# Gate/up weights from six raw tiles, three of them lent, and second attention's weights prepared one tile at a time by whole-tile operations

## The chip, the cores and the metric

The kernel runs on one core of a Trainium2 chip. The metric is the device time of one launch in microseconds, the median of several runs; lower is better.

## The reference, cut to what matters

A two-layer decoder over 1024 tokens of width 1024, float32. Layer A is differential attention, layer B stick-breaking attention with keys and values of its own from the residual stream. Behind each attention stand an output projection and a SwiGLU feed-forward block of inner width 2816, each with root-mean-square norms before and after and a residual sum.

```python
def swiglu(h, w_gate_up, w_down):
    gate, up = jnp.split(h @ w_gate_up, 2, axis=-1)
    return (jax.nn.silu(gate) * up) @ w_down

kv = rms_norm(x, kv_norm_g) @ kv_w            # layer B: keys and values
q  = rms_norm(x, mix_pre_g[1]) @ b_w_q        # layer B: queries
x  = x + rms_norm(m @ b_w_o, mix_post_g[1])   # layer B: output projection
```

## The kernel before, in words

**Products.** Each float32 operand is cut into a rounded high part and a remainder, and every product is three matmuls (high by high, low by high, high by low) into one PSUM bank.

**Order of the work.** The kernel is written as threads (Python generators). A planner, `Weaver`, runs them against a clock of its own and gives every instruction its place in the queue of its engine; each engine then works strictly in that order on the chip, SyncE's queue of DMA issues (SP) too. The planner's costs stand in the code: three matmuls of 512 columns take 1536/2372 us (`pe_time`), a DVE operation of n columns (1.04 n + 70) ns, an ACT one (0.833 n + 52) ns, plus 93 ns with a scale from a tile. A load is thought to be there 2.6 us behind its issue of 1.0 us, and a store's tile free 2.4 us behind its own. Tiles come from pools (`Slots`): `acq` waits in the planner until one is free, `put` gives it back, `lend` and `unlend` move tiles from one pool to another for a time.

**Gate/up.** `phase_ffn` runs twice ("A", "B"). Its loop `gate_up` goes over 22 column blocks f. For each, seven operand combinations (order `MORD`, a Strassen-like scheme over gate and up weights and the two halves of the tokens) give seven products of 12 matmuls, 84 matmuls for one f. `take` adds each product from its bank to half tiles `e` on DVE, `gated` makes silu(gate) times up, and `store` writes the result to DRAM (`act`).

**Gate/up's weights.** One `QuadJob` for each f. `loader` acquires three tiles of the pool `S_raw` (two are loaded with gate and up weights of 512 KB each, one is work space) and spawns `quad`. That makes seven split weight tiles `w` (pool `S_w`, nine tiles): DVE forms the combinations that need one (two as `raw<-raw`, three as `raw<-raw,raw`), ACT casts the high part, POOL subtracts to get the low part. Only when all seven are done do the three raw tiles go back. `S_raw` has three tiles, so the loads of the next f stand behind the last POOL subtraction of this f.

**Second attention's weights.** `pre_weights` prepares 32 weight tiles for layer B while feed-forward A runs: 24 with a gain for each 128-column block (queries, keys, values) and 8 without (`wo`). Each job takes two of the five tiles of pool `S_tr` (`tr`; the norms between stages use the same tiles), loads 512 KB, splits and stores both parts to DRAM (`prebq`, `prebk`, `prebv`, `prewo`). With a gain, the split is 8 ACT and 8 DVE operations of 128 columns. The next job is begun 1.0 + 2.6 + 13.5 us of the planner's time behind the last, so two jobs can be in work.

**Down.** `down` follows gate/up with 22 split rows of the down weight (`Job`, also through `S_raw`), its sums in tiles `acc` and `e`.

Of the kernel before, what the change touches and what calls it, by code (L numbers as in the profile page):

```python
# [13 lines left out]
AF = mybir.ActivationFunctionType  # L14
ALU = mybir.AluOpType
# [3 lines left out]
P = 128  # L19
# [3 lines left out]
NC = D // P  # L23
# [10 lines left out]
MORD = (3, 5, 4, 2, 6, 7, 1)  # L34
# [207 lines left out]
def acq(*homes):  # L242
    return ("acq", homes)


def delay(t):
    return ("delay", t)
# [10 lines left out]
def ACT(n, extra=0):  # L258
    return ("act", (0.833 * n + 52 + 93 * extra) / 1e3)


def DVE(n, rate=1.04):
    return ("dve", (rate * n + 70) / 1e3)
# [6 lines left out]
def SP(x=0.62):  # L270
    return ("sp", x)
# [17 lines left out]
def yoco_trunk(  # L289
# [7 lines left out]
    W = Weaver()  # L297
    pe, act, dve, pool, sp = [InOrder(tc, e) for e in (nc.tensor, nc.scalar, nc.vector, nc.gpsimd, nc.sync)]
# [8 lines left out]
    def tiles(pl, n, shape, dt, name):  # L307
        return [pl.tile(shape, dt, name=f"{name}{i}") for i in range(n)]
# [13 lines left out]
    S_raw = Slots(tiles(cpool, 3, [P, 1024], F32, "raw"))  # L322
    S_tr = Slots(tiles(cpool, 5, [P, 1024], F32, "tr"))
# [7 lines left out]
    oB = drp.tile([D, T], F32, name="oB")  # L331
    actd = [drp.tile([P, T], F32, name=f"act{f}") for f in range(NF)]

    S_half, S_trx = Slots(), Slots()

    def halves(t):
        return [t[:, :512], t[:, 512:]]
# [47 lines left out]
    pres = []  # L385

    def pre_weights(ready):
        yield ready
        yield delay(25.0)

        def work(job, raw, hi):
            if job.gain is not None:
                g_ev, g = job.gain()
                yield g_ev
            h = hi.t.bitcast(F32R)
            if job.gain is not None:
                for c in range(NC):
                    cs = slice(c * P, c * P + P)
                    yield ACT(P, 1)
                    act.activation(h[:, cs], raw.t[:, cs], AF.Copy, scale=g[:, c:c + 1])  # L400
                for c in range(NC):
                    cs = slice(c * P, c * P + P)
                    yield DVE(P + 58)
                    dve.scalar_tensor_tensor(raw.t[:, cs], raw.t[:, cs], g[:, c:c + 1], hi.t[:, cs],
                                             op0=ALU.mult, op1=ALU.subtract)
            else:
                yield ACT(1024)
                act.copy(h, raw.t)
                yield DVE(1024)
                dve.tensor_tensor(raw.t, raw.t, hi.t, op=ALU.subtract)  # L410

            def store(x, cs):
                yield SP(1.0)
                sp.dma_start(out=job.d[:, cs], in_=x.t)
                yield delay(2.4)
                W.put(x)
                W.set(job.ev)

            W.spawn(store(hi, slice(0, 1024)), 60, "prest")
            W.spawn(store(raw, slice(1024, 2048)), 60, "prest")  # L420

        for job in pres:
            raw = yield acq(S_tr)
            hi = yield acq(S_tr)
            yield SP(1.0)
            sp.dma_start(out=job.view(raw.t), in_=job.src)
            yield delay(2.6)
            W.spawn(work(job, raw, hi), 60, "pre" + job.name)
            yield delay(13.5)

    def loader():
        queue = []
# [86 lines left out]
        def load(k_, job):  # L519
            yield turn[k_]  # L520
            home = job.home if job.home is not None else S_w
            sh = yield acq(home)
            sl = yield acq(home)
            W.set(turn[k_ + 1])
            yield job.pre.ev
            for x, cs in ((sh, slice(0, 1024)), (sl, slice(1024, 2048))):
                yield SP(1.0)
                sp.dma_start(out=f32(x.t), in_=job.pre.d[:, cs])
            yield delay(2.6)
            job.h, job.l = sh, sl  # L530
            W.set(job.ev)

        for k, job in enumerate(jobs):
            W.cur.prio = -2 if k > 3 else 3
            if isinstance(job, LoadJob):
                if job.after is not None:
                    yield job.after
                W.spawn(load(k, job), -2, "load" + job.name)
                continue
            if isinstance(job, QuadJob):  # L540
                rr = []
                for src in job.srcs:
                    raw = yield acq(S_raw)
                    yield SP(1.0)
                    sp.dma_start(out=cview(raw.t)[0], in_=src.rearrange("(c p) n -> p c n", p=P))
                    rr.append(raw)
                rr.append((yield acq(S_raw)))
                yield delay(2.6)
                W.spawn(quad(k, job, *rr), plan("p.splitg", 20), "quad" + job.name)
                yield delay(-2.6)  # L550
                continue
            if job.after is not None:
                yield job.after
            raw = yield acq(S_raw)
            n = 0
            for src, view in job.srcs:
                yield SP(1.0 if len(job.srcs) == 1 else 0.5)
                dst, n = view(raw.t)
                sp.dma_start(out=dst, in_=src)
            yield delay(2.6)  # L560
            W.spawn(split(k, job, raw, n), plan("p.split" + job.name[0], 20) if k > 3 else -3, "split" + job.name)
            yield delay(-2.6)
# [266 lines left out]
    hA, hFA, hB, hFB = Hid(), QuadHid(), Hid(), QuadHid()  # L829
    phase_done = {k: Ev() for k in ("A", "woA", "ffnA", "B", "woB", "ffnB")}  # L830
# [746 lines left out]
    def phase_ffn(nm, st, before, hin, xsrc, xdst, g_post, hout):  # L1577
# [7 lines left out]
        def opener():  # L1585
            yield phase_done[before]
            gL, plL = phase_pool("ffl" + nm)
            W.give(S_act, tiles(plL, 4, [P, 1024], F32R, "fa"))
            gG, plG = phase_pool("gu" + nm, "right")
            own = tiles(plG, 6, [P, 4, 512], F32R, "hx")  # L1590
            W.spawn(hin.combine(own), -20, "combine")
            W.spawn(scratch(), -20, "scratch")
            W.set(opened)
            yield gu_done
            gG.__exit__(None, None, None)
            g, pl = phase_pool("dn" + nm, "right")
            acc.extend(tiles(pl, 2, [P, D], F32, "acc"))
            for x in hin.e:
                v = x.rearrange("p a b -> p (a b)")
                acc.extend([v[:, :1024], v[:, 1024:]])  # L1600
            stv["gpost"] = pl.tile([P, D], F32, name="gpostf")
            stv["junk"] = pl.tile([P, 1024], BF16, name="junkf")
            W.give(S_act, tiles(pl, 8, [P, 1024], F32R, "fb"))
            stv["gev"] = Ev()
            W.spawn(load_bcast(stv["gpost"], g_post, stv["gev"]), 6)
            W.set(dn_open)
            yield left
            g.__exit__(None, None, None)
            hin.gE.__exit__(None, None, None)
            gL.__exit__(None, None, None)  # L1610
            W.set(phase_done["ffn" + nm])

        W.spawn(opener(), -30, "open")
        W.spawn(hin.ready(), 0, "ready")

        def scratch():
            for i, x in ((6, hin.e[2]), (7, hin.e[1]), (1, hin.e[0])):
                yield hin.op_ev[i]
                v = x.rearrange("p a b -> p (a b)")
                W.give(S_sg, [v[:, k * 512:(k + 1) * 512] for k in range(4)])  # L1620
# [499 lines left out]
    def main():  # L2120
        W.spawn(warm_up(), 0, "warm")
        W.spawn(first_norm(), -37, "first")
        W.spawn(loader(), -2, "loader")
        W.spawn(load_gA(), -13, "gA")
        W.spawn(load_gB(), 35, "gB")
        W.spawn(phase_A(), -77, "A")
        W.spawn(phase_wo("A", sA, "A", oA, x_in, xd[0], mix_post_g[0], ffn_pre_g[0], hFA, eA), 49, "woA")
        W.spawn(load_early(eA, "A", oA, lambda m: [oA_ev[h][m // 4] for h in range(7)], sA), -47, "earlyA")
        W.spawn(wo_early("A", sA, eA), 75, "earlyMM")
        W.spawn(wo_early("B", sB, eB), 81, "earlyMM")  # L2130
        W.spawn(phase_ffn("A", fA, "woA", hFA, xd[0], xd[1], ffn_post_g[0], hB), 26, "ffnA")
        W.spawn(pre_weights(phase_done["woA"]), 60, "pre")
        W.spawn(phase_B(), 1, "B")
        W.spawn(phase_wo("B", sB, "B", oB, xd[1], xd[2], mix_post_g[1], ffn_pre_g[1], hFB, eB), -5, "woB")
        W.spawn(load_early(eB, "B", oB, lambda m: [oB_ev[p][m // 2] for p in range(7)], sB), -41, "earlyB")
        W.spawn(phase_ffn("B", fB, "woB", hFB, xd[2], out_f, ffn_post_g[1], None), -80, "ffnB")
        return
        yield
# [40 lines left out]
```

## Time and profile before

| | us |
|---|---|
| median of 3 runs | 2670.67 (2669.65 to 2674.35) |
| profiled execution, own time | 2676.72 |
| its span, first to last instruction | 2674.9 |

PE is the matmul engine, DVE the vector, ACT the scalar engine, POOL GpSimd, SPq the queue that issues the DMAs. All helpers record one source line, so groups are told apart by their tiles: `bank<-hT,w` and `bank<-hx,w` are gate/up's matmuls (48 and 36 for one f), `bank<-w,fa` and `bank<-w,fb` the down product's, `tr<-tr,gB` the preparation of second attention's weights. Behind a group stands the idle time of its engine just before it and, after `<-`, what ended that.

### The profile page before, as it was taken

What the parts mean: (1) busy time and instruction counts of PE and PEld (TensorE: products, weight loads), DVE (VectorE), ACT (ScalarE), POOL (GpSimd) and SP (SyncE); (2) the same over time, 40 slices, a digit from 0 to 9 for tenths busy, and PEclk for the clock granted to TensorE, in tenths of its full rate; (3) what the DMA queues carried; (4) which work ended last, traced back from release to release, by engine and by line L of the source; (5) the groups of instructions that cost most, each with busy time, mean ns of one, the idle gap of its engine ahead of it and who ended that gap; (6) DMA issues with size and microseconds to landing.
All of it is one profiled execution on the core that took longest, in us unless ns stands there. A gap on an engine that the chain in (4) does not pass through costs nothing. (4 is left out here: it accounts for less than half of the span.)

```text
span 2674.9 us, 36855 instructions
## 1 busy us (share of the span) xinstructions
PE 2549.2 (95%) x12771; PEld 2153.7 (81%) x12771; DVE 1857.0 (69%) x3351; ACT 1189.3 (44%) x2710; POOL 776.2 (29%) x713
## 2 busy tenths in 40 slices
PE   8999999897999999899999999999989999999998
PEld 8998999675887777688878888887767888888887
DVE  4767676866766666676768887888777655564667
ACT  4555555644444444331146655556454333332111
POOL 2111111334444444323210000000044545453331
PEclk9999999998999999999999999999999999999999
DMA  6333333441444444555454344444542232324233
GB/s 168 87 80 80 92 76 97 127 163 55 142 155 152 157 150 142 205 189 185 154 195 110 104 118 113 116 116 127 189 144 78 81 95 71 95 71 152 100 102 127
DMA packets 259258, 331.55 MB, mean 124 GB/s; under 512 B 20992, under 2 KB 179072, under 8 KB 259072
## 3 DMA queue, kind: packets, MB, share of 16 engines
q1 hardware_dynamic: 259072, 329.20, 40.1%
q8 instruction: 101, 1.65, 0.3%
q14 instruction: 85, 0.70, 0.1%
HBM read 197.67 MB, written 81.13 MB: 104 GB/s over the span
## 5 line engine op out<-in xcount | busy, mean ns | idle before, releaser
L283 PE MATMUL bank<-hT,w 128*128 128x512 f32 x3264 | 814.1, 399 | 26.0 <-ACT w L283 12.9
L283 PEld LDWEIGHTS bank<-hT,w 128*128 128x128 f32 x3264 | 607.7, 191 | 158.8 <-ACT w L283 18.3
L283 POOL TENSOR_TENSOR w<-raw,w 128x512 fp32r<-128x512 f32 (+1 forms) x343 | 522.1, 1539 | 514.8 <-ACT w L283 450.6
L283 PE MATMUL bank<-hx,w 128*128 128x512 f32 x1584 | 367.6, 389 | 4.7 <-DVE hx L283 4.7
L283 DVE TENSOR_TENSOR e<-e,bank 128x512 f32<-128x512 f32 x360 | 240.7, 680 | 187.1 <-ACT e L283 100.0
L283 PEld LDWEIGHTS bank<-hx,w 128*128 128x128 f32 x1584 | 296.9, 188 | 68.3 <-DVE hx L283 6.9
L283 PE MATMUL bank<-w,hT 128*128 128x384 f32 (+1 forms) x1728 | 344.6, 346 | 4.8 <-DMA w<-prewo 2.6
L283 ACT CAST w<-raw 128x512 fp32r<-128x512 f32 x308 | 188.1, 618 | 353.2 <-DVE raw L283 222.9
L283 PE MATMUL bank<-w,fb 128*128 128x512 f32 x1344 | 311.5, 389 | 1.2 <-POOL w L283 1.0
L283 PEld LDWEIGHTS bank<-w,hT 128*128 128x128 f32 x1728 | 299.7, 189 | 15.0 <-DMA w<-prewo 3.1
L283 PEld LDWEIGHTS bank<-w,fb 128*128 128x128 f32 x1344 | 252.0, 188 | 54.3 <-POOL w L283 1.5
L283 DVE TENSOR_TENSOR e<-bank,e 128x512 f32<-128x512 f32 x224 | 151.8, 687 | 90.5 <-PE bank L283 87.9
L283 PE MATMUL bank<-ident,tr 128*128 128x128 f32 x1059 | 163.6, 282 | 42.8 <-DVE tr L283 22.3
L283 PE MATMUL bank<-w,fa 128*128 128x512 f32 x768 | 186.0, 396 | 11.1 <-DVE e L283 5.9
L283 PEld LDWEIGHTS bank<-ident,tr 128*128 128x128 f32 x1059 | 129.8, 145 | 76.1 <-DVE tr L283 25.9
L283 PEld LDWEIGHTS bank<-w,fa 128*128 128x128 f32 x768 | 145.9, 191 | 43.7 <-ACT e L283 5.2
L283 POOL MEMSET atB<- 128x128 f32 x128 | 25.1, 205 | 504.3 <-PE bank L283 499.4
L283 POOL TENSOR_SCALAR w<-raw 128x1024 fp32r<-128x1024 f32 x48 | 68.9, 1435 | 300.3 <-PE bank L283 210.2
L283 DVE TENSOR_TENSOR raw<-raw 128x512 f32<-128x512 f32 x88 | 59.5, 713 | 120.7 <-DMA raw<-in_ffn_w_gate_up_dram 120.7
L283 POOL TENSOR_TENSOR sm<-sm,nhalf 128x1 f32<-128x1 f32 (+1 forms) x72 | 57.7, 802 | 291.0 <-DVE sm L283 291.0
L283 DVE TENSOR_TENSOR_SCAN rB<-rB,zeroB 128x512 f32<-128x512 f32 (+3 forms) x144 | 134.9, 951 | 7.8 <-ACT rB L283 6.9
L283 DVE TENSOR_TENSOR raw<-raw,raw 128x512 f32<-128x512 f32 x132 | 131.8, 998 | 0.0
(210 smaller groups left out, 3618.8 us busy)
## 6 DMA issues: line engine op xcount, KB each, us to landing
raw<-in_ffn_w_gate_up_dram SPq DMA_DIRECT2D x88, 512.0 KB, 5.1
xy<-st SPq DMA_DIRECT2D x192, 128.0 KB, 2.3
act<-e SPq DMA_DIRECT2D x88, 256.0 KB, 5.5
raw<-in_ffn_w_down_dram SPq DMA_DIRECT2D x44, 512.0 KB, 4.5
xyB<-stB SPq DMA_DIRECT2D x176, 128.0 KB, 4.2
fb<-act SPq DMA_DIRECT2D x28, 512.0 KB, 4.4
raw<-in_a_w_qkv_dram SPq DMA_DIRECT2D x96, 128.0 KB, 2.6
tr<-x SPq DMA_DIRECT2D x22, 512.0 KB, 4.1
```

What stands on the lines that cost most here:

```text
L283: return tc.keep_in_program_order(f(*a, **k))
```

## The change

The gate/up jobs may take their raw tiles from `S_raw` or from a new pool `S_rx`. In each feed-forward block, once all seven operands of the tokens are ready, three of the five `tr` tiles are lent to `S_rx`, and they go back when gate/up ends. `pre_weights` now starts at that same point rather than 25 us behind the end of the output projection. With two `tr` tiles left it has one job in work. A job with a gain is now one DVE multiplication of 1024 columns in place, then, as for one without, one ACT cast and one DVE subtraction of 1024 columns. Its pause falls from 13.5 to 11.0 us.

```diff
-    S_half, S_trx = Slots(), Slots()
+    S_half, S_trx, S_rx = Slots(), Slots(), Slots()
 ...
     def pre_weights(ready):
-        yield ready
-        yield delay(25.0)
+        for ev in ready:
+            yield ev
 ...
             if job.gain is not None:
-                for c in range(NC):
-                    cs = slice(c * P, c * P + P)
-                    yield ACT(P, 1)
-                    act.activation(h[:, cs], raw.t[:, cs], AF.Copy, scale=g[:, c:c + 1])
-                for c in range(NC):
-                    cs = slice(c * P, c * P + P)
-                    yield DVE(P + 58)
-                    dve.scalar_tensor_tensor(raw.t[:, cs], raw.t[:, cs], g[:, c:c + 1], hi.t[:, cs],
-                                             op0=ALU.mult, op1=ALU.subtract)
-            else:
-                yield ACT(1024)
-                act.copy(h, raw.t)
+                v3 = raw.t.rearrange("p (c n) -> p c n", c=NC)
                 yield DVE(1024)
-                dve.tensor_tensor(raw.t, raw.t, hi.t, op=ALU.subtract)
+                dve.tensor_tensor(v3, v3, g.unsqueeze(2).broadcast_to([P, NC, P]), op=ALU.mult)
+            yield ACT(1024)
+            act.copy(h, raw.t)
 ...
+            yield DVE(1024)
+            dve.tensor_tensor(raw.t, raw.t, hi.t, op=ALU.subtract)
 ...
-            yield delay(13.5)
+            yield delay(11.0)
 ...
-                    raw = yield acq(S_raw)
+                    raw = yield acq(S_raw, S_rx)
 ...
-                rr.append((yield acq(S_raw)))
+                rr.append((yield acq(S_raw, S_rx)))
 ...
+            bookR = []
+            W.spawn(lend_raw(bookR), -20, "lendraw")
             W.set(opened)
             yield gu_done
+            W.unlend(bookR)
 ...
+        def lend_raw(book):
+            for i in MORD:
+                yield hin.op_ev[i]
+            yield from W.lend(S_tr, S_rx, 3, whole, book)
 ...
-        W.spawn(pre_weights(phase_done["woA"]), 60, "pre")
+        W.spawn(pre_weights([hFA.op_ev[i] for i in MORD]), 60, "pre")
```

## Rows read from the trace of the kernel before

**Rows 1.** The page, busy time and share of the span.
```profile
PE 2549.2 (95%) x12771; PEld 2153.7 (81%) x12771; DVE 1857.0 (69%) x3351; ACT 1189.3 (44%) x2710; POOL 776.2 (29%) x713
```

**Rows 2.** Windows by stage: length, busy by engine, PEclk, DMA share, GB/s.
```profile
785.76:1109.17 323.41, 301.64 (x1261) 240.04 (x1260) 219.85 (x343) 141.01 (x314) 150.15 (x108) 0.97 0.45 148
1109.17:1146.94 37.77, 26.71 (x96) 20.30 (x97) 20.65 (x31) 18.57 (x39) 7.26 (x5) 0.86 0.65 236
1146.94:1321.02 174.08, 174.08 (x769) 144.15 (x768) 127.08 (x171) 30.80 (x41) 54.73 (x29) 1.00 0.53 186
2028.67:2428.51 399.84, 399.84 (x1765) 331.08 (x1764) 229.29 (x315) 152.24 (x269) 212.34 (x147) 1.00 0.30 92
```

**Rows 3.** Timeline of PE, gate/up A: start, length, group.
```profile
728.52 11.04 PE L283 MATMUL bank<-hT,w 128*128 128x512 f32 x48
...
747.56 11.04 PE L283 MATMUL bank<-hT,w 128*128 128x512 f32 x48
...
893.48 0.73 PE L283 MATMUL bank<-hT,w 128*128 128x512 f32 x2 [1.69 <-ACT w L283]
...
1100.85 8.32 PE L283 MATMUL bank<-hx,w 128*128 128x512 f32 x36
```

**Rows 4.** Timeline of the DMA queue SP in gate/up A.
```profile
668.93 0.99 SPq L283 DMA_DIRECT2D raw<-in_ffn_w_gate_up_dram  x2
...
798.23 1.01 SPq L283 DMA_DIRECT2D raw<-in_ffn_w_gate_up_dram  x2
...
905.95 1.01 SPq L283 DMA_DIRECT2D raw<-in_ffn_w_gate_up_dram  x2
907.01 1.07 SPq L283 DMA_DIRECT2D tr<-in_kv_w_dram  x1
...
927.17 1.01 SPq L283 DMA_DIRECT2D raw<-in_ffn_w_gate_up_dram  x2
```

**Rows 5.** Waits of SP, 785.76 to 1099: total us, times, longest.
```profile
SPq L283 <- POOL w L283: 204.8, 14, 15.6
```

**Rows 6.** Timeline of all engines within one period of gate/up A.
```profile
911.93 1.29 DVE L283 TENSOR_TENSOR raw<-raw 128x512 f32<-128x512 f32 x2 [3.27 <-DMA raw<-in_ffn_w_gate_up_dram]
...
922.17 1.70 DVE L283 SCALAR_TENSOR_TENSOR tr<-tr,gB,tr 128x128 f32<-128x128 f32 x2
...
925.86 1.29 POOL L283 TENSOR_TENSOR w<-raw,w 128x512 fp32r<-128x512 f32 x1 [2.13 <-ACT w L283]
```

**Rows 7.** Groups of 785.76 to 1109.17: busy, mean ns, idle before.
```profile
L283 DVE SCALAR_TENSOR_TENSOR tr<-tr,gB,tr 128x128 f32<-128x128 f32 x120 | 77.6, 685 | 0.0
...
L283 ACT ACTIVATE tr<-tr,gB 128x128 fp32r<-128x128 f32 x120 | 43.3, 397 | 15.4 <-DMA tr<-in_kv_w_dram 11.4 <-DMA tr<-in_b_w_q_dram 3.9
```

**Rows 8.** 1024-column operations: DVE and ACT on tr (min/median/max ns), DVE on w.
```profile
L283 DVE TENSOR_TENSOR tr<-tr,tr x8: 1214/1218/1466, 1189.9 to 1316.4; 128x1024 f32<-128x1024 f32 x8
...
L283 ACT CAST tr<-tr x8: 1047/1053/1057, 1181.5 to 1310.6; 128x1024 fp32r<-128x1024 f32 x8
...
L283 DVE TENSOR_TENSOR w<-raw,w 128x1024 fp32r<-128x1024 f32 x6 | 14.2, 2359 | 0.0
```

**Rows 9.** DMA issues, us to landing: first two gate/up A, last two down A.
```profile
prebq<-tr SPq DMA_DIRECT2D x10, 512.0 KB, 7.1
tr<-in_kv_w_dram SPq DMA_DIRECT2D x10, 512.0 KB, 7.2
...
prebk<-tr SPq DMA_DIRECT2D x2, 512.0 KB, 3.6
...
tr<-in_kv_w_dram SPq DMA_DIRECT2D x1, 512.0 KB, 4.8
```

**Rows 10.** Timeline at the end of gate/up A: two rows of ACT, one of PE.
```profile
1108.78 0.40 ACT L283 ACTIVATE tr<-tr,gB 128x128 fp32r<-128x128 f32 x1 [6.10 <-DMA tr<-in_kv_w_dram]
...
1113.39 4.46 PE L283 MATMUL bank<-w,fa 128*128 128x512 f32 x12 [4.22 <-DVE e L283]
...
1136.15 0.40 ACT L283 ACTIVATE tr<-tr,gB 128x128 fp32r<-128x128 f32 x1 [3.38 <-DMA tr<-in_b_w_q_dram]
```

## The prediction

> **What bounds the kernel now.** The page comes first: PE is busy 95% of the span [rows 1], so all its gaps together are 126 us, and the question is in which stage they lie. The windows by stage answer it [rows 2]. Gate/up B and the body of the down product A have no PE gap at all. Gate/up A from 785.8 us on and the 38 us behind it are the stages with gaps that the change can reach.
>
> The timeline of PE gives their size [rows 3]. An undisturbed f takes 747.56 - 728.52 = 19.04 us, 0.2267 us a matmul. The last 15 f run from 785.76 to 1100.85 + 8.32 = 1109.17, 323.4 us where 15 x 19.04 = 285.6 would do: **37.8 us lost**, a mean period of 21.56 us. Each f starts with a wait such as 1.69 us for ACT's cast of the weights, and after some of them the granted clock is lower (0.97 in the mean of the stretch [rows 2]). In the 37.77 us behind it, 96 matmuls are done, 21.8 us at 0.2267: **16.0 us lost** at the change-over to the down product.
>
> SP's timeline tells why [rows 4]. Gate/up loads are issued every (798.23 - 668.93)/6 = 21.55 us, from the very start; PE ran at 19.04 up to 785.8 on the split tiles it had ahead and then fell to SP's pace. In front of the loads SP waits for POOL's last subtraction of the f before, 204.8 us in 14 waits [rows 5]. So the three raw tiles make a loop [rows 4, 6]: load issued at 905.95, landed at 911.93 (6.0 us), splits until POOL's last one ends at 925.86 + 1.29 = 927.15, next load at 927.17. The 15.2 us of splits contain DVE's short operations on `tr` between the combinations (1.70 us for two at 922.17). The planner meant otherwise: it charges 0.263 us for one of these and thinks a load is there 3.6 us after its issue begins; the trace has 0.685 [rows 7] and 6.0. Its f takes 28 x 1536/2372 = 18.13 us.
>
> **The change part by part.**
>
> *Six raw tiles.* With a second set the loads of f+1 wait for the f before the last one, so they can be issued up to a whole period (19 us) sooner, and the 6.0 us landing has that long to hide in. What stays in sequence for one f is the splitting, at most 15.2 us, under 19.04. The loop therefore stops setting the pace and PE does: 15 x (21.56 - 19.04) = 37.8 us to win. I take 34, since the waits at single loads need not all go. In gate/up B the same is worth 0: PE is busy 399.84 of 399.84 us there. Lending issues no instruction; its cost is that `tr` is short, below.
>
> *Wide operations.* Per job with a gain ACT goes from 8 x 0.397 = 3.2 us [rows 7] to one cast of 1.05 [rows 8], DVE from 8 x 0.685 = 5.5 us to two operations of 1024 columns. DVE's price has two ends in the trace: 1.22 us each while POOL rests (`tr<-tr,tr` in down A) and 2.36 (`w<-raw,w`, beside POOL's own subtractions) [rows 8]. I take 1.5, as POOL is busy 150 of 323 us [rows 2], under half. So DVE saves 5.5 - 3.0 = 2.5 us a job (0.8 at the dear end), in the loop that is gone anyway. The Trainium skill, "SBUF — State Buffer", Who interferes with whom, says that a DVE operation with two SBUF inputs and a GpSimd operation that reads SBUF exclude each other for a whole instruction, so that a long operation gains less than its length promises. By that rule, with 2.36 for both operations, the loop of the next part would be 16.8 us rather than 15.05, which is the first rival. The rows bear it out so far as POOL is at work.
>
> *One job in work.* Here the change adds a wait. A load of `tr` now stands on SP behind the landing of both stores of the job before, where two jobs alternated. Behind it on SP stand gate/up's loads and the `act` stores, and through the loads ACT, DVE, POOL and PE. DVE's multiplication waits for the load to land, where ACT did (15.4 us over 15 jobs [rows 7]); behind it on DVE stand the additions that free PE's banks. The loop of one job: landing of the load between 4.8 us (down A) and 7.2 (gate/up A) [rows 9], multiplication 1.22 to 2.36, cast 1.05, subtraction 1.22 to 2.36, three issues 1.0 (1.07 for one behind two others [rows 4]; I take a third of it for each), landing of the stores 3.6 to 7.1 [rows 9]. Its ends are 12.9 and 21.1 us. I take 5.5 + 1.5 + 1.05 + 1.5 + 1.0 + 4.5 = **15.05 us**, nearer to down A's landings, since in gate/up A the load of `tr` is issued right behind a pair of gate/up loads that one POOL wait released [rows 4, 5], and that wait goes. The planner puts jobs 1.0 + 2.6 + 11.0 = 14.6 us apart, 18.13/14.6 = 1.242 for one f, and so allows 19.04/1.242 = 15.3 us in the trace's time. So it just fits, at a price of 0, with no room: where the loop takes C, f takes 1.242 C. The lead of split tiles covers the first slips; before, it covered six periods of 2.5 us, 15 us, and I take the same again.
>
> *Earlier start, shorter pause.* 32 jobs at 14.6 us are 467 us of the planner's time against 22 x 18.13 = 399 of gate/up, so some 27 are done in gate/up A (before, one for each f, 15 in 15 periods by the 120 operations of [rows 7]). The five left are without a gain and lie beside the down product, where PE has no gaps [rows 2]: 0.
>
> *The change-over.* ACT was held 6.10 us at 1108.78 for a load of `tr`, then DVE's additions came late and PE waited 4.22 us; ACT was held again for 3.38 us at 1136.15 [rows 10]. Both are the preparation's, and DVE is behind PE at that point because of the loop. Gate/up B passes into its down product with no gap. A job may still stand there, so of 16.0 us I take 6, with ends 0 and 16.
>
> *Order elsewhere.* All later instructions are planned anew from a shifted clock. I take 0, with ends of 6 us either way, about the size of one change-over's stall.
>
> **Sum.** 34 + 6 = 40 us off the profiled execution's 2676.72 gives 2636.7. That execution lies 6.05 us above the median shown, so the forecast is 2670.67 - 40 = **2631 us**. If all of 37.8 and 16.0 goes and the order helps by 5, it is 2612.
>
> **The rivals.**
>
> *The one-job loop holds part.* With C = 16.5 us, f would take 20.5 us: 21 x 1.45 - 15 = 15.5 us lost against 37.8 before, and the change-over stays as it was, since DVE is behind again. That gains 22: **2648 us**. For it: the planner thinks stores free their tile 2.4 us on and the trace has at least 3.6 [rows 9]. Against it: the transfers no longer come in one burst. Chance 0.14.
>
> *The change-over or a later stage takes a third or more back.* Gate/up A ends 34 us sooner, but down's first weights are loaded and split as they were; the DMA share is already 0.65 there [rows 2]. The 16 us grow to 30: 34 - 14 = 20, **2651 us**. Against it: gate/up B changes over with no loss in the same code. Chance 0.06.
>
> *Slower: the one-job loop becomes the bound.* The point where it decides is where gate/up A loses as much as before: 21 x (1.242 C - 19.04) - 15 = 37.8, C = 17.4 us. That needs landings like those in gate/up A now and DVE operations that each meet POOL, with the ends above 21.1. At C = 18: 21 x 3.32 - 15 = 54.6 us lost, 17 more than before: **2688 us**. For it: the landings of 7.2 and 7.1 us. Against it: they were seen right behind pairs of gate/up loads, and a slower loop spaces the transfers out. Chance 0.13.
>
> *No change.* C between 17.2 and 17.6, or the change doesn't do what it says: the nine weight tiles, not the raw ones, decide when the next f is split, the loads come earlier and nothing else does. SP's 204.8 us of waiting for POOL speak against it. **2668 us**, chance 0.07.
>
> **How the numbers follow.** The forecast has 0.60, with 2612 to 2648 as its own range. Faster by over 0.2% (5.3 us, about what a measurement of this kernel can tell from no change) is 0.60 + 0.14 + 0.06 = 0.80, within 0.07, slower 0.13. The range for 8 in 10 runs from 2612, everything won, to 2668, the case without change; the slower case lies outside.
>
> **What would show it.** Right: gate/up A's f at 19.04 us from first to last, its loads issued well before POOL's last subtraction of the f before, SP's waits for POOL w far under 204.8 us, the `tr` group on DVE in rows of 1024 columns with means of 1.2 to 1.8 us, and landings of `tr` and `pre` DMAs under 6 us. The first rival: f between 19.5 and 21 us, SP waiting for a `pre` store in front of each `tr` load, and DVE for a load of `tr`. The slower one: the same with tr loads 18 us or more apart. The prediction is wrong if f stays near 21.5 us, or if the stages behind gate/up A lose what it gains.

## The result and the profile after

The changed kernel takes 2624.33 us (median of four runs, 2621.18 to 2625.57) against 2672.51 of the kernel before beside it; the ratio is 0.9818, 95% interval 0.9801 to 0.9835. That is 48 us off (44 to 53), where 40 were forecast. Its profiled execution takes 2625.28 us with a span of 2623.5, 51.4 under the one of before.

The windows of the changed kernel for the same stages as in [rows 2] (length, then busy time by engine, PEclk, DMA share, GB/s):

```profile
785.39:1070.99 285.60, 285.60 (x1262) 236.49 (x1260) 222.47 (x256) 125.70 (x207) 159.53 (x105) 1.00 0.58 191
1070.99:1094.90 23.91, 22.09 (x97) 17.94 (x96) 8.71 (x9) 14.09 (x22) 1.48 (x2) 1.00 0.64 221
1094.90:1268.98 174.08, 174.08 (x769) 144.14 (x768) 120.78 (x152) 22.63 (x22) 53.77 (x29) 1.00 0.41 142
...
1976.00:2376.00 400.00, 400.00 (x1765) 331.17 (x1766) 241.29 (x316) 156.67 (x269) 193.72 (x147) 1.00 0.30 91
```

The last 15 f of gate/up A take 285.6 us, which is 15 x 19.04 to a tenth, with PE busy all the time at the full granted clock. The body of down A has its 174.08 us again, and PE is as full in gate/up B as it was. PE's timeline has one gap left in the whole stretch:

```profile
975.79 11.04 PE L283 MATMUL bank<-hT,w 128*128 128x512 f32 x48
...
994.83 11.04 PE L283 MATMUL bank<-hT,w 128*128 128x512 f32 x48
...
1062.83 8.32 PE L283 MATMUL bank<-hx,w 128*128 128x512 f32 x36
1070.99 13.76 PE L283 MATMUL bank<-w,fa 128*128 128x512 f32 x60
1086.57 8.50 PE L283 MATMUL bank<-w,fa 128*128 128x512 f32 x36 [1.82 <-ACT e L283]
```

994.83 - 975.79 is 19.04 us. At the change-over the first row of `fb` comes at 1094.90, 23.75 us behind the end of gate/up (1062.83 + 8.32 = 1071.15), where it was 37.77; 21.8 would be without loss. So 16.0 us of loss have become 2.0.

SP's queue, to be laid beside [rows 4]:

```profile
899.58 1.01 SPq L283 DMA_DIRECT2D tr<-in_ffn_w_gate_up_dram  x2
900.68 1.72 SPq L283 DMA_DIRECT2D tr<-in_b_w_q_dram  x1
...
910.28 1.58 SPq L283 DMA_DIRECT2D prebq<-tr  x2
918.05 1.01 SPq L283 DMA_DIRECT2D raw<-in_ffn_w_gate_up_dram  x2
919.15 1.38 SPq L283 DMA_DIRECT2D tr<-in_kv_w_dram  x1
```

Gate/up's loads now go to `raw` and to lent `tr` tiles in turn. SP's waits between 785.39 and 1070.99 (total us, times, longest):

```profile
SPq L283 <- ACT tr L283: 83.9, 16, 8.9
SPq L283 <- POOL w L283: 66.0, 14, 8.2
...
SPq L283 <- DMA prebk<-tr: 4.7, 4, 1.6
SPq L283 <- DMA prebv<-tr: 3.8, 2, 2.7
SPq L283 <- DMA prebq<-tr: 2.7, 2, 1.6
```

It still waits for POOL, but 66.0 us rather than the 204.8 of [rows 5], and PE, busy for 285.60 of 285.60 us, never feels it. SP's largest wait is a new one: 83.9 us for ACT's cast of a `tr` tile, in front of the store of that tile. The wait that the prediction named, for the landing of a job's own stores, is 11.2 us in 8 waits. Landings in the same stretch, beside the first two of [rows 9]:

```profile
prebk<-tr SPq DMA_DIRECT2D x12, 512.0 KB, 3.3
...
tr<-in_kv_w_dram SPq DMA_DIRECT2D x11, 512.0 KB, 4.6
...
prebq<-tr SPq DMA_DIRECT2D x10, 512.0 KB, 2.7
...
tr<-in_b_w_q_dram SPq DMA_DIRECT2D x5, 512.0 KB, 5.2
```

### The profile page after: what moved, and what is told of

Read it like the earlier page. It is cut to its first block, busy times and chain, and to the rows that moved or that the text cites. A ratio compares the mean times of both kernels' runs of the same rounds, so it can differ in the third digit from the quotient of the medians.

```text
span 2623.5 us, 36666 instructions
## 1 busy us (share of the span) xinstructions
PE 2529.2 (96%) x12771; PEld 2148.9 (82%) x12771; DVE 1866.4 (71%) x3207; ACT 1165.2 (44%) x2542; POOL 774.8 (30%) x713
## 5 line engine op out<-in xcount | busy, mean ns | idle before, releaser
L283 PE MATMUL bank<-hT,w 128*128 128x512 f32 x3264 | 799.9, 395 | 4.5 <-DMA w<-prebq 3.0
L283 POOL TENSOR_TENSOR w<-raw,w 128x512 fp32r<-128x512 f32 (+1 forms) x203 | 324.2, 1606 | 296.0 <-ACT w L283 235.8
L283 POOL TENSOR_TENSOR w<-tr,w 128x512 fp32r<-128x512 f32 x140 | 198.6, 1428 | 177.0 <-ACT w L283 168.5
L283 ACT CAST w<-raw 128x512 fp32r<-128x512 f32 x168 | 103.4, 622 | 186.9 <-DVE raw L283 155.9
L283 ACT CAST w<-tr 128x512 fp32r<-128x512 f32 x140 | 85.9, 620 | 140.8 <-DVE tr L283 133.9
L283 ACT COPY e<-bank 128x512 f32<-128x512 f32 x180 | 101.3, 588 | 102.2 <-PE bank L283 102.1
```

The source lines that it names most:

```text
L283: return tc.keep_in_program_order(f(*a, **k))
```

## The experiments

One table serves them all. It is made from PE's timeline of each kernel's profile: **gate/up A** from its first matmul behind the opening transposes to its last end; **change-over** from there to the first `fb` (21.8 without loss); **to B** from there to the first `hT,w` of attention B; **B** from there to the first full f of gate/up B; **rest** to the end of the span. All in us. Each row is one profiled execution, and 21.8 us of the change-over are PE's own work.

```
kernel              gate/up A  change-over  to B     B        rest
before              457.27     37.77        226.87   654.86   646.23
changed             419.55     23.75        226.66   655.63   646.31
wide only           448.65     36.76        227.04   652.15   646.32
lent, narrow        419.54     22.88        228.57   656.44   646.29
no extra raw        446.91     33.26        226.62   655.32   646.29
lend two            419.50     23.62        226.73   657.05   646.24
lend one            424.51     29.18        226.65   655.40   646.29
lend in A only      419.54     23.29        226.65   656.04   646.55
pause 7             419.54     26.74        227.08   654.70   646.30
pause 12            419.51     21.60        226.95   653.48   646.26
pause 13.5          419.52     23.52        227.63   653.84   646.30
pause 16            419.51     21.60        223.82   673.55   646.26
```

What is left out is the part ahead of gate/up A, which the change doesn't reach; it ends between 647.7 and 653.4 us from run to run.

**Wide operations alone.** The kernel before with the new `work` of `pre_weights` and nothing else:

```diff
-                for c in range(NC):
-                    act.activation(h[:, cs], raw.t[:, cs], AF.Copy, scale=g[:, c:c + 1])
...
+                dve.tensor_tensor(v3, v3, g.unsqueeze(2).broadcast_to([P, NC, P]), op=ALU.mult)
+            act.copy(h, raw.t)
```

> The kernel before with the whole-tile operations alone: three raw tiles, two jobs in work, start and pause as before. Theory 'landing' (the 6.0 us landing of the loads inside the three-tile loop is what sets 21.56 us): the loop sheds only the narrow DVE operations that stand between the combinations, about 1 to 2 us, f comes to 19.6 to 20.6 us and the time to 2640 to 2655. Rival 'narrow operations' (the eight DVE operations that take 0.685 us where the planner counts 0.263 are what sets it): the 2.5 us a job come off the loop in full, f is 19.1 us or less and the time 2622 to 2632.

It took 2665.51 us, ratio 0.9984 (0.9973 to 0.9994): both theories expected too much. SP's timeline and DVE's row of the landing in this kernel:

```profile
906.58 1.01 SPq L283 DMA_DIRECT2D raw<-in_ffn_w_gate_up_dram  x2
...
912.16 1.30 DVE L283 TENSOR_TENSOR raw<-raw 128x512 f32<-128x512 f32 x2 [4.45 <-DMA raw<-in_ffn_w_gate_up_dram]
...
925.77 1.30 POOL L283 TENSOR_TENSOR w<-raw,w 128x512 fp32r<-128x512 f32 x1 [1.33 <-ACT w L283]
...
927.10 1.01 SPq L283 DMA_DIRECT2D raw<-in_ffn_w_gate_up_dram  x2
```

The loop is still there, 5.6 us of landing and 14.9 of splits; its mean over 14 periods is 21.04 us (loads at 778.34 and 1072.89) against 21.55. The groups between 785 and 1094 us (busy, mean ns, idle before) tell where the saving went, first those of the kernel before, then those of this one:

```profile
L283 POOL TENSOR_TENSOR w<-raw,w 128x512 fp32r<-128x512 f32 x103 | 143.8, 1409 | 171.9 <-ACT w L283 156.5 <-PE bank L283 14.5
...
L283 DVE TENSOR_TENSOR raw<-raw,raw 128x512 f32<-128x512 f32 x44 | 37.9, 861 | 0.0
...
L283 DVE TENSOR_TENSOR e<-e 128x512 f32<-128x512 f32 x28 | 19.2, 685 | 1.4
```

```profile
L283 POOL TENSOR_TENSOR w<-raw,w 128x512 fp32r<-128x512 f32 x105 | 171.3, 1655 | 144.2 <-ACT w L283 136.6 <-PE bank L283 7.6
...
L283 DVE TENSOR_TENSOR raw<-raw,raw 128x512 f32<-128x512 f32 x45 | 51.6, 1147 | 0.0
L283 DVE TENSOR_TENSOR tr<-tr,tr 128x1024 f32<-128x1024 f32 x15 | 33.1, 2205 | 7.7 <-ACT tr L283 7.7
L283 DVE TENSOR_TENSOR tr<-tr,gB 128x1024 f32<-128x1024 f32 x15 | 26.7, 1780 | 11.8 <-DMA tr<-in_kv_w_dram 9.8 <-DMA tr<-in_b_w_q_dram 2.0
...
L283 DVE TENSOR_TENSOR e<-e 128x512 f32<-128x512 f32 x29 | 22.2, 803 | 0.0
```

The pair costs 1.78 + 2.21 = 3.99 us a job beside POOL, so 1.5 off the 5.5 of [rows 7]; and the combinations that gate/up's splits stand on went to 1.147 us each, where they were 0.861 in the same window of before: 3 x 0.29 = 0.9 given back in each period. POOL's subtractions, which end the loop, went from 1.409 to 1.655 us as well; how the loss divides between the two was not tried.

**Lending with the narrow operations.** The changed kernel with the old `work` put back (the diff above, reversed). One job in work, the early start and the pause of 11.0 us stay in it; lending by itself was not run.

> The changed kernel with the eight ACT and eight DVE operations of 128 columns put back: six raw tiles, one job in work. Theory 'landing': the loads are out of the loop, f is 19.04 us unless the longer one-job loop (about 2 us more of work) holds it; 2622 to 2640. Rival 'narrow operations': gate/up A stays slow, f over 20.5 us, 2648 or more.

2625.20 us, ratio 0.9832 (0.9817 to 0.9847); gate/up A 419.54 us. The theory of the landing holds, and the whole gain is there without the wide operations. The longer one-job loop did not show. Between 785 and 1070.9 us SP's wait for POOL and DVE's `e<-e` products are:

```profile
SPq L283 <- POOL w L283: 149.9, 15, 11.6
```

```profile
L283 DVE TENSOR_TENSOR e<-e 128x512 f32<-128x512 f32 x30 | 19.3, 680 | 0.1
```

So SP can wait 149.9 us for POOL with PE at its full pace: what counts is that the loads land before their f needs them, and the fall of that wait to 66.0 us in the changed kernel is no measure of the gain.

**No extra raw tiles.** The changed kernel, three tiles still lent, but not taken:

```diff
-                    raw = yield acq(S_raw, S_rx)
+                    raw = yield acq(S_raw)
```

(the same in the line of the work tile.)

> The changed kernel whose gate/up jobs don't take the lent tiles: three raw tiles, one job in work, whole-tile operations, early start and short pause. Theory 'landing': SP waits for POOL's last subtraction again, f 19.6 to 20.8 us, 2640 to 2658. Rival 'narrow operations': as the changed kernel, 2622 to 2632.

2656.96 us, ratio 0.9950 (0.9933 to 0.9966). As the theory had it: f is 20.68 us by SP's loads (774.69 to 1064.14, 14 periods) and gate/up A 446.9 us. SP's loads, POOL's last subtraction and DVE's row of the landing:

```profile
918.43 1.01 SPq L283 DMA_DIRECT2D raw<-in_ffn_w_gate_up_dram  x2
...
924.12 1.29 DVE L283 TENSOR_TENSOR raw<-raw 128x512 f32<-128x512 f32 x2 [4.56 <-DMA raw<-in_ffn_w_gate_up_dram]
...
938.19 1.30 POOL L283 TENSOR_TENSOR w<-raw,w 128x512 fp32r<-128x512 f32 x1 [1.61 <-ACT w L283]
...
939.52 1.46 SPq L283 DMA_DIRECT2D raw<-in_ffn_w_gate_up_dram  x2
```

The loop of before is there again, 5.7 us of landing and 15.4 of splits in this period. So the wide operations, one job in work, the early start and the short pause together are worth some 14 us, and the extra tiles the other 33. These parts don't add up with the full gain of the kernel with narrow operations: what makes the loop shorter is worth nothing once PE sets the pace. The three parts other than the wide operations were not taken out one by one, but for the pause, below.

**Two tiles lent.**

```diff
-            yield from W.lend(S_tr, S_rx, 3, whole, book)
+            yield from W.lend(S_tr, S_rx, 2, whole, book)
```

> Two tiles lent rather than three. Theory 'landing': both loads of the next f can go ahead and only the work tile waits, so the landing is out of the loop and the time is that of the changed kernel, 2619 to 2632, f 19.04 us. Rival (a whole second set is needed): the jobs still wait for the last subtraction, f above 19.5 us, 2635 or more.

2623.38 us, ratio 0.9826 (0.9811 to 0.9840), gate/up A 419.50 us. Two tiles do what three do; a whole second set is not needed, only room for both loads.

**One tile lent.** The same line with 1.

> One tile lent: four raw tiles for gate/up. Theory 'landing': one of the two loads goes ahead, the other still waits for the last subtraction of the f before, so its landing stays in the loop and the time is that of three raw tiles, 2648 to 2660, f 20 to 21 us. Rival (any spare tile loosens the loop): 2624 to 2640.

2635.08 us, ratio 0.9868 (0.9853 to 0.9882): faster than the theory's 2648 to 2660, within the rival's range. SP's loads and DVE's row of the landing:

```profile
908.38 0.38 SPq L283 DMA_DIRECT2D raw<-in_ffn_w_gate_up_dram  x1
908.81 0.57 SPq L283 DMA_DIRECT2D tr<-in_ffn_w_gate_up_dram  x1
...
912.44 1.29 DVE L283 TENSOR_TENSOR raw<-raw 128x512 f32<-128x512 f32 x2 [2.94 <-DMA raw<-in_ffn_w_gate_up_dram]
...
928.27 1.01 SPq L283 DMA_DIRECT2D raw<-in_ffn_w_gate_up_dram  x2
```

By the order of `acq`, the first of the two issues at 908.4 is this f's second load and the other is the next f's first, a period early. DVE's first combination reads the second load of its f. So the mechanism is the expected one, a load still in the loop; but that load is now first in the queue and is there 912.44 - 908.38 = 4.06 us behind the issue, where as the second of a pair it took 5.6 to 6.0 us from the pair's issue. With 15.8 us of splits that gives about 19.9 us here, and 19.47 in the mean of 15 periods (752.16 to 1044.19), half a microsecond above PE's pace, which the lead nearly covers: gate/up A loses 5 us, and the change-over 7.4.

**Lending in feed-forward A alone.**

```diff
-            W.spawn(lend_raw(bookR), -20, "lendraw")
+            if nm == "A":
+                W.spawn(lend_raw(bookR), -20, "lendraw")
```

> The changed kernel that lends in feed-forward A alone. Theory: gate/up B was at PE's pace with three raw tiles, so lending there is worth nothing: 2621 to 2628, ratio to the kernel before 0.981 to 0.983. Rival (six raw tiles help B's start or change-over): over 2630.

2623.95 us, ratio 0.9826 (0.9811 to 0.9840): nothing is won or lost in feed-forward B, as forecast.

**The pause between jobs.** Four values in place of 11.0 in `yield delay(11.0)`. First the rival of the prediction that would have made the kernel slower, the one-job loop:

> The changed kernel with a pause of 7.0 rather than 11.0 us: the planner spaces the jobs by its own idea of the one-job loop (about 13 to 13.6 us, 1.33 to 1.39 jobs for one f). Theory 'the one-job loop takes 15.05 us', as in the prediction: f = 20.0 to 20.9 us once the lead is used up, 6 to 25 us lost in gate/up A, 2630 to 2649. Rival (the loop is shorter than the estimate, under 13.7 us): nothing lost, 2619 to 2629, the jobs 13 to 14 us apart with PE at 19.04.

2628.35 us, ratio 0.9843 (0.9828 to 0.9858), gate/up A 419.54 us. SP's loads of the first job and of the 24th:

```profile
672.06 2.52 SPq L283 DMA_DIRECT2D tr<-in_b_w_q_dram  x1
...
1001.74 0.42 SPq L283 DMA_DIRECT2D tr<-in_kv_w_dram  x1
```

(1001.74 - 672.06)/23 = 14.33 us a job, with PE at its full pace. The loop of one job is 14.3 us or less, so the 15.05 of the prediction was too long, and the 17.4 us at which the rival begins lay at least 3.1 us off rather than 2.35. The 3 us that this kernel lost against an expected 0 lie in the change-over (26.74), where PE waits twice for ACT.

> The changed kernel with a pause of 16.0 us, under one job for one f (0.93), so some 11 jobs are left for the down product. Theory (PE is the bound of gate/up A, the pace of the jobs is worth nothing so long as the loop fits): 2620 to 2630. Rival (the shorter pause is part of the gain, since the jobs left over hold ACT and DVE at the change-over or the later stage): 2632 to 2645.

2638.02 us, ratio 0.9872 (0.9856 to 0.9889). The time is the rival's, the mechanism is neither's: gate/up A is at PE's pace, the change-over has no loss, the stretch to B is 3 us shorter (eight transposes, about 1 us of it, fall behind its end), and 18 us are lost in **B**. The rival's jobs left over are not the cause: the last stores of a job are issued at 1324.47, and what is lost lies in output projection B, from 1900 us on. PE's timeline has waits there that the changed kernel lacks:

```profile
1907.58 5.49 PE L283 MATMUL bank<-w,ow 128*128 128x512 f32 x12 [6.28 <-DVE trl L283]
...
1925.13 1.09 PE L283 MATMUL bank<-ident,trx 128*128 128x128 f32 x8 [2.05 <-DVE trx L283]
...
1933.06 1.97 PE L283 MATMUL bank<-ident,tr 128*128 128x128 f32 x8 [1.83 <-DVE tr L283]
```

The whole kernel has the same 12771 matmuls; the planner, whose clock the pause has moved, dealt the norms and transposes of that stage out in another order. Waiting is not all of the loss: behind the first wait 12 matmuls take 5.49 us, where the changed kernel's 12 of the same kind at 1893.38 take 2.88. The last 128 us of B, in the changed kernel and in this one, have PEclk 0.96 and 0.89:

```profile
1849.19:1977.19 128.00, 115.99 (x550) 94.48 (x549) 93.86 (x134) 63.40 (x121) 38.87 (x38) 0.96 0.41 143
```

```profile
1863.84:1991.84 128.00, 106.56 (x476) 85.48 (x477) 87.00 (x124) 58.29 (x110) 40.92 (x37) 0.89 0.41 142
```

Two further pauses were to tell whether the pause or the order is the cause:

> The changed kernel with a pause of 12.0 us: the same work, jobs 15.6 us apart in the plan. Theory (the 14 us that a pause of 16.0 cost lie in output projection B, which the planner dealt out in another order, not in the pace of the jobs): gate/up A at 19.04 us for one f, and later stages either as in the changed kernel or re-dealt, 2619 to 2640, with any difference over 4 us found behind 1840 us. Rival (each us of pause costs by the jobs left over): 2626 to 2629, the difference at the change-over or in down A.

> The changed kernel with the pause of the kernel before, 13.5 us. Theory (re-dealt order): as for 12.0, any difference over 4 us lies behind 1840 us, and the times need not rise with the pause. Rival (the pause itself): 2630 to 2633, between the pauses of 11.0 and 16.0, the difference ahead of 1400 us.

A pause of 12.0 took 2620.35 us, ratio 0.9803 (0.9788 to 0.9817), one of 13.5 took 2625.42, ratio 0.9822 (0.9806 to 0.9839). The time does not rise with the pause: 2628, 2624, 2620, 2625, 2638 for 7, 11, 12, 13.5 and 16. Gate/up A is the same in all five; the change-over varies by 5 us and stage B by 20. The theory's place was missed at 12.0: of the 5.8 us by which its profiled span is the shorter, 2.2 lie in B, 2.2 at the change-over and the rest ahead of gate/up A. So the pause itself is ruled out as a cost that grows, and the order stays as the likely cause; which detail of it costs the 18 us at 16.0 was not tried. The kernel with 12.0 is the fastest of all, 4 us under the changed one by medians, but the two intervals overlap, and nothing says that 12.0 is better than 11.0 for a reason that lasts.

## Why the prediction was right

The direction, the range and the mechanism held: three raw tiles closed a loop of landing and splitting, and with room for the next loads PE sets the pace. By its steps:

- *Six raw tiles*, 34 of 37.8 us: all came, 457.27 - 419.55 = 37.7. It comes with the narrow operations too, and no kernel without the extra tiles has it (446.9 and 448.7).
- *The change-over*, 6 of 16.0 with an end at 16: 14.0 came. This is the term of the sum that was mis-sized. The prediction named two causes, ACT's waits for a load of `tr` and a DVE that is behind because of the loop, and priced it as if the first would mostly stay. The table ties it to the loop: 11 to 16 us are lost where the loop sets the pace (before, wide only, no extra raw), 7 with one tile lent, 0 to 5 where PE does. In the first four PE waits there for DVE's additions (4.22 us in [rows 10]); in the others it waits for ACT alone, or not at all. The longest of these waits is that of wide only:

```profile
1110.64 18.28 PE L283 MATMUL bank<-w,fa 128*128 128x512 f32 x66 [9.21 <-DVE e L283]
```

  What makes the 0 to 5 us among the kernels at PE's pace was not tried.
- *Wide operations*, 2.5 us a job saved on DVE "in the loop that is gone anyway": worth nothing here, as the sum had it; but their price was taken for the operations alone. Alone in the old loop they brought 0.5 us a period, as the splits beside them became slower. In the changed kernel they cost 1.42 and 1.28 us, near the 1.5 taken, and the `e<-e` products, silu(gate) times up, become slower. DVE's groups of 785.39 to 1070.99:

```profile
L283 DVE TENSOR_TENSOR e<-e 128x512 f32<-128x512 f32 x30 | 39.0, 1336 | 0.3 <-ACT e L283 0.2
L283 DVE TENSOR_TENSOR tr<-tr,tr 128x1024 f32<-128x1024 f32 x19 | 24.2, 1276 | 3.1 <-ACT tr L283 3.1
L283 DVE TENSOR_TENSOR tr<-tr,gB 128x1024 f32<-128x1024 f32 x17 | 24.1, 1418 | 12.7 <-DMA tr<-in_kv_w_dram 6.5 <-DMA tr<-in_b_w_q_dram 6.1
```

  The `e<-e` products take 1.336 us here and 0.680 with the narrow operations put back, the only difference between the two kernels. The time is 2625.2 with those all the same.
- *One job in work*, 15.05 us against 15.3 allowed, price 0: right that it fits, too long in size. Loads landed in 4.6 and 5.2 us (keys and values, queries) and stores in 2.7 to 3.9, below the 5.5 and 4.5 taken. That the transfers no longer come in one heap would explain it but was not tried by itself; with the wide operations alone the stores already land in 2.6 to 3.0 us. At 14.33 us a job PE still lost nothing in gate/up A.
- *Order elsewhere*, 0 with ends of 6 us: 0.8 us lost in stage B here, which is luck: the ends were too narrow. One number in the planner moved that stage by 18 us, and a third of this change's gain could have gone that way with no mechanism at fault.

Together 37.7 + 14.0 less 0.8 and some tenths are the 51 us between the two profiled executions. The medians are 48 us apart: the execution profiled before lies 4.2 us above its median, the changed one 1.0.

## What to carry to other kernels

Where a buffer's next load waits for the last reader of the same buffer, add landing and reading time and hold the sum against the pace of the engine that should be the bound; here 6.0 + 15.2 against 19.04, and room for the two loads alone, two tiles of 4 KB a partition, was worth all of the gain. A lead built up earlier hides such a loop at first (six f ran at full pace), so read the period on the queue, not on the busy engine, and count the debt that is paid at the next change of stage. In a kernel whose whole order comes from one planned clock, an edit can deal later stages out anew; compare stage by stage before giving a cause the difference.

## What was not expected of the hardware

Fewer and longer DVE operations did not shorten DVE's work beside a busy POOL: over 14 periods DVE is busy 207.56 us in wide only (778.34 to 1072.89) and 206.42 in the kernel before (777.24 to 1077.93). Merging sixteen of 128 columns into three of 1024 (two of them on DVE) raised the combinations of two SBUF tiles from 0.861 to 1.147 us and the `e<-e` products from 0.685 to 0.803 with three raw tiles, to 1.336 in the changed kernel, where the narrow ones leave them at 0.680. The Trainium skill, "SBUF — State Buffer", Who interferes with whom, says that a DVE operation with two SBUF inputs contends with a GpSimd operation that reads SBUF, and calls their shared port pair an exclusive lock. These rows fit that, and the additions from a PSUM bank, which have one SBUF input, stayed at 0.676 to 0.685 us in the four kernels compared here; that the port is the cause was not tried by itself.

The 512 KB load that DVE's first combination reads was there 4.06 us behind its issue when it went first, and 5.6 to 6.0 us behind the pair's issue when it went second.
